# A hybrid decoder block on one core: an own PSUM bank for query, key and mLSTM transposes, another order of the Strassen products in the paired projections, and a pause in the sums of the feed-forward modulation

## The chip, the core and the metric

The kernel runs on one core of a Trainium2 chip. A core has five engines with a queue each: PE (TensorE) multiplies matrices and writes its results to PSUM, DVE (VectorE) and ACT (ScalarE) do elementwise work and move PSUM results to SBUF, POOL (GpSimd) does some elementwise work and SP (SyncE) issues the DMA transfers. Each engine works through its queue in order, and semaphores make one engine wait for another. The metric is the time of one execution on the device, in microseconds (us); lower is better.

## The reference

A decoder block over 2048 tokens of width 1024, all in float32. Cut to what matters:

```python
mod = c @ w_ada + b_ada
shift_m, scale_m, gate_m, shift_f, scale_f, gate_f = split(mod, 6)
h = rms_norm(x, g_pre_mix) * (1 + scale_m) + shift_m
q_a, k_a, v_a, q_m, k_m, v_m, o_m, i_m, f_m, g_a, g_m = split(h @ w_in)
y_a = sliding_window_attention(rope(q_a), rope(k_a), v_a, sinks)      # 8 heads, 2 key heads, window 128
q_m, k_m = split(silu(causal_depthwise_conv([q_m, k_m])))
y_m = sigmoid(o_m) * head_layer_norm(mlstm_chunkwise(q_m, k_m, v_m, i_m + b_i, f_m + b_f))
merged = sigmoid(g_a) * (y_a @ w_branch_attn) + sigmoid(g_m) * (y_m @ w_branch_mlstm)
x = x + gate_m * rms_norm(merged @ w_out, g_post_mix)
h2 = rms_norm(x, g_pre_ffn) * (1 + scale_f) + shift_f
x = x + gate_f * rms_norm((silu(h2 @ w_gate) * (h2 @ w_up)) @ w_down, g_post_ffn)   # width 2816
```

## The kernel before

**Stages.** Phase 1 computes the mixers in two superblocks of two token blocks each (b0 and b1, 512 tokens a block); phase 2 is the feed-forward network over two halves of 1024 tokens. In a superblock the projections of queries, of keys and values (`q_kv`) and of the mLSTM values (`vm`) come first for b0 and then for b1. Then come 14 *pairs*, which are projections of both blocks at once (output gates, mLSTM queries and keys, branch gates), with the mLSTM woven in after the pair ("qk", 3), and then the branch and output projections (`outputs`). Each float32 operand of a large product is split into two parts, hi and lo, and three products of parts make one: `split` makes `whi` on ACT (L256, L259) and `wlo` on DVE (L257, L260) for weights, and the token operands are split by `hprep` (L521 to L537) and `hsums` (L552) for the mixers.

**Pairs.** A pair multiplies a 2 by 2 arrangement of weight quarters with one of token quarters by seven products in place of eight (Strassen, Winograd's form). `PROD` lists the seven in order, each as a weight operand and a token operand (S and T are sums of quarters). `pair_parts` issues them: 12 matmuls of 128x512 a product. Products 0, 2, 4 and 6 accumulate in one PSUM bank X, which is read on the way; products 1, 3 and 5 each take a bank of their own. `combine` evacuates: ACT copies, DVE adds (L1511 and the lines by it). In phase 1 there are 28 pairs, in the feed-forward 44 (22 for each half, gate and up). The `down` projection has its own list, `DOWN`.

**PSUM.** There are eight banks of 128 partitions by 2 KB. Four belong to the tag `acc` (`acc_tile`), four to the tag `mix` (`mix_tile`), from which everything else is served: scores and PV products of attention, all transposes, mLSTM, the second bank of the feed-forward pairs and of `down`. A bank is given again only when what was in it has been read.

**Attention.** `attention(n)` works on one tile of 128 queries. It loads `at`, which holds the queries and keys that `q_stream` and `k_stream` wrote to DRAM (`at_d`). For two halves `jj` it takes two banks, one for each key head `g`; the score matmuls use rows 0 to 63 of the array for one head and 64 to 127 for the other, and are written in alternation. ACT copies (L931) and DVE masks (L933) the scores, DVE and ACT make maxima, exponentials and sums, POOL multiplies by the reciprocal sum (L950), then PE transposes the result and multiplies with the values. `q_stream` and `k_stream` take rotated queries and keys, transpose them into a bank (`pt`), and have ACT and DVE (L772, L798) split them.

**Order.** The program is written with generators: `run2` walks the parts of the main stream, prepares weights ahead of their use, and at each step `tick` moves on the side streams (`spawn`) whose delays have run out on a simulated clock. A framework then schedules the written program onto the engines with a timeline of its own, from tile pools and their free banks, so a changed pool changes the order of instructions on every engine. `ada_stream` (L452) is such a side stream: it computes the modulation vectors, one weight load and one DVE multiply-add (L428) a term, 16 terms a vector. For scale, shift and gate of the feed-forward (48 terms) it starts ahead of the output projection of the first block.

Of the kernel before, what the change touches and what calls it, by code (L numbers as in the profile page):

```python
# [10 lines left out]
F32 = mybir.dt.float32  # L11
# [8 lines left out]
P = 128  # L20
# [30 lines left out]
ADA_AHEAD = (1, 3, 4)  # L51

# [19 lines left out]
def decoder_block(ctx: ExitStack, tc: tile.TileContext, a: dict, out: bass.AP, dbg=None):  # L72
# [26 lines left out]

    def mix_tile():  # L100
        return ps_mix.tile([P, 512], F32, tag="mix", name=nm("mix"))
# [634 lines left out]
    def superblock(sb):  # L736
# [27 lines left out]
        def q_stream(b, t, yz):  # L764
            yield L_ROPE
            y, z = yz
            pt = mix_tile()
# [23 lines left out]
        def k_stream(n, yz):  # L791
            yield L_ROPEK
            y, z = yz
            pt = mix_tile()
# [206 lines left out]
        def chunk_state(c):  # L1001
# [13 lines left out]
            pk = mix_tile()  # L1015
# [26 lines left out]
        def chunk_out(c):  # L1042
# [43 lines left out]
            py = mix_tile()  # L1086
# [124 lines left out]
        def outputs(b):  # L1211
# [41 lines left out]
            def before_out():  # L1253
                if b == 0:
                    finish(R["ada_m"])
                    R_ada.append(spawn(ada_stream([(4, "scale"), (3, "shift"), (5, "gate")], 9000.0)))
# [30 lines left out]
        yield lambda: hps.update(t=spawn(hsums(("T2", "T4"))))  # L1287
# [37 lines left out]
    R_ada = []  # L1325

# [8 lines left out]
    PROD = (("11", "11"), ("12", "21"), ("S2", "T2"), ("22", "T4"), ("S1", "T1"), ("S3", "T3"), ("S4", "22"))  # L1335
# [42 lines left out]
    def h_combine(b2, rows, quarters, sums):  # L1378
# [14 lines left out]
        for k in range(4):  # L1393
            xk = xn
            v = {}
            for j, (half, i) in enumerate(QUADS):
                kk = k + 4 * half
                ps = mix_tile()
# [67 lines left out]
    def pair_parts(w, c0, done, new, spare, bank):  # L1466
# [4 lines left out]
        def make(i, prep):  # L1471
            B = PROD[i][1]

            def mms(wt):
                hi, lo = quad(wt[0]), quad(wt[1])
                if i in IN_X:
                    if i == 0:
                        R["X"] = acc_tile()
                    ps = R["X"]
                else:  # L1480
                    ps = bank()
                for kk in range(4):
                    l, r = (hi[:, kk, :], lo[:, kk, :]), tuple(t[:, kk, :] for t in HC[B])
                    mm(ps, l[0], r[0], kk == 0 and i in (0, 1, 3, 5), False, True)
# [4 lines left out]
            return Part(raw, prep, mms, weave=bank is not mix_tile, ahead=4)  # L1489
# [4 lines left out]
    def combine(i, ps, R, new, done):  # L1494
        if i == 0:
            R["P1"] = new()
            A.copy(R["P1"], ps)
        elif i == 1:
            V.tensor_tensor(R["P1"], ps, R["P1"], op=ALU.add)
            done("11", R["P1"], False)  # L1500
        elif i == 2:
            R["U2"] = new()
            A.copy(R["U2"], ps)
        elif i == 3:
            V.tensor_tensor(R["U2"], ps, R["U2"], op=ALU.add)
        elif i == 4:
            R["U4"] = new()
            A.copy(R["U4"], ps)
        elif i == 5:
            V.tensor_tensor(R["U2"], ps, R["U2"], op=ALU.add)  # L1510
            V.tensor_tensor(R["U4"], ps, R["U4"], op=ALU.add)  # L1511
            done("21", R["U2"], False)
            done("22", R["U4"], False)
# [46 lines left out]
    def gate_up(b2):  # L1560
        late = None
        for p in range(NP):
# [27 lines left out]
            gp, up = (list(pair_parts(w, p * 256, done, unit, unit, mix_tile)) for w, done in ((wg, done_g), (wu, done_u)))  # L1590
# [33 lines left out]
    DOWN = (("11", "11"), ("S3", "T3"), ("S2", "T2"), ("22", "T4"), ("S1", "T1"), ("12", "21"), ("S4", "22"))  # L1624
    HELD = 4

    def down(b2):
# [105 lines left out]
        def make(raw, i, p, j):  # L1733
# [16 lines left out]
            def mms(ab):  # L1750
                if p == 0:
                    for t in range(NT):
                        if i == 0:
                            R[t]["X"] = acc_tile()
                        if i not in IN_X:
                            R[t]["Y"] = mix_tile()
# [113 lines left out]
```

## Time and profile before

| what | value |
|---|---|
| median of 3 runs | 2710.72 us (2709.86 to 2713.3) |
| profiled execution, own time | 2716.59 us |
| its span | 2714.9 us |
| PE busy | 2639.2 us, 97% |
| DVE busy | 1986.2 us, 73% |
| ACT busy | 1299.8 us, 48% |
| DMA | 511.90 MB moved |

The profile is of one execution. It names each instruction by line of the kernel, engine, operation and tiles (out<-in, the numbers of the buffers left out), with partitions and elements and how often it ran. "Idle before" is the time an engine stood before an instruction, and the releaser is what ended that wait. The granted clock is TensorE's, as a share of full speed.

### The profile page before, as it was taken

Reading aid. Unit: us, or ns where it says so; the run is one execution under the profiler, and the core shown is the slowest. Engines: PE = TensorE matmul, PEld = TensorE weight load, DVE = VectorE, ACT = ScalarE, POOL = GpSimd, SP = SyncE. Lnnn points to the kernel's source line nnn. Section 1 sums busy time; section 2 is a strip of 40 time slices with the busy share of each in tenths; the row PEclk is TensorE's granted clock in tenths of the full one; section 3 lists DMA queues with packets and bytes.
Section 4 is the critical chain, followed back from the end, with each engine's and each line's share of the span. In section 5 each row is a group of like instructions: output and inputs, shape, how many; then the busy total and the mean of one; then the engine's idle time right before and its main releaser. Section 6 shows DMA issues by size and latency. Waiting matters only on the chain.

```text
span 2714.9 us, 35793 instructions
## 1 busy us (share of the span) xinstructions
PE 2639.2 (97%) x12310; PEld 2138.9 (79%) x12310; DVE 1986.2 (73%) x3906; ACT 1299.8 (48%) x2558; POOL 148.2 (5%) x189
## 2 busy tenths in 40 slices
PE   6989999999998999999999999999999999999998
PEld 4867788888885678888887888888877888888886
DVE  7968788778695778876687777776677676766456
ACT  5556544444755564444563443335554333333444
POOL 2010001100101000110000000000000000000000
PEclk8999999999998999999999999999999999999999
DMA  7654355897574544678765564436675232324566
GB/s 249 206 184 157 128 172 179 269 340 248 196 235 147 196 138 138 213 231 291 251 224 198 175 201 152 155 113 213 215 271 188 97 117 86 113 97 144 186 210 217
DMA packets 353639, 511.90 MB, mean 189 GB/s; under 512 B 25120, under 2 KB 213660, under 8 KB 348208
## 3 DMA queue, kind: packets, MB, share of 16 engines
q1 hardware_dynamic: 353456, 509.61, 56.9%
q8 instruction: 97, 1.59, 0.2%
q14 instruction: 86, 0.70, 0.1%
HBM read 357.12 MB, written 144.02 MB: 185 GB/s over the span
## 4 chain that ended last, share of the span: by engine, by line
PE 85%; DVE 7%; DMA 4%; ACT 2%; issue 1%; POOL 0%; SPq 0%; DVEq 0%; ACTq 0%; POOLq 0%
PE acc L204 61%; PE mix L204 22%; PE mix L209 2%; DVE hl L1357 1%; DVE tm L428 1%; DMA raw<-as_d 1%; ACT tm L946 1%; ACT hl L1356 1%; DMA raw<-in_w_in_dram 1%; DMA at_d<-tx 0%; DMA big<-in_x_dram 0%; DVE wlo L260 0%; DMA tx<-in_w_ada_dram 0%; DVE w L1667 0%; DMA at<-at_d 0%
## 5 line engine op out<-in xcount | busy, mean ns | idle before, releaser
L204 PE MATMUL acc<-big,hl 128*128 128x512 f32 x3936 | 940.8, 394 | 4.3 <-ACT tx L827 1.8
L204 PEld LDWEIGHTS acc<-big,hl 128*128 128x128 f32 x3936 | 733.3, 188 | 172.5 <-issue 13.8
L1356 ACT CAST hl<-raw 128x512 fp32r<-128x512 f32 x732 | 440.1, 621 | 493.4 <-PE acc L204 222.2
L1357 DVE TENSOR_TENSOR hl<-raw,hl 128x512 fp32r<-128x512 f32 x732 | 496.3, 694 | 194.8 <-ACT hl L1356 194.0
L204 PE MATMUL acc<-whi,big 128*128 128x512 f32 (+1 forms) x1280 | 379.3, 377 | 10.8 <-ACT big L518 8.4
L204 PEld LDWEIGHTS acc<-whi,big 128*128 128x128 f32 x1280 | 236.2, 192 | 52.4 <-ACT big L518 8.5
L204 PE MATMUL mix<-big,hl 128*128 128x512 f32 x1056 | 263.9, 391 | 1.7 <-ACT hl L1356 1.1
L204 PE MATMUL acc<-wlo,big 128*128 128x512 f32 (+1 forms) x640 | 241.2, 379 | 6.4 <-DVE wlo L260 6.4
L204 PE MATMUL acc<-hl,hl 128*128 128x512 f32 x1008 | 237.4, 393 | 5.1 <-DVE hl L1357 3.4
L204 PEld LDWEIGHTS mix<-big,hl 128*128 128x128 f32 x1056 | 197.9, 188 | 45.9 <-ACT hl L1356 1.9
L204 PEld LDWEIGHTS acc<-hl,hl 128*128 128x128 f32 x1008 | 187.0, 188 | 50.9 <-DVE hl L1357 8.8
L204 PE MATMUL mix<-hl,hl 128*128 128x512 f32 x792 | 182.7, 391 | 1.3 <-DVE hl L1357 0.9
L204 PEld LDWEIGHTS mix<-hl,hl 128*128 128x128 f32 x792 | 147.9, 188 | 35.3 <-DVE hl L1357 3.1
L204 PE MATMUL acc<-big,whi 128*128 128x512 f32 x512 | 157.4, 393 | 0.0
L260 DVE TENSOR_TENSOR wlo<-raw,whi 128x1024 fp32r<-128x1024 f32 (+1 forms) x96 | 109.0, 1137 | 65.5 <-ACT whi L259 59.8
L259 ACT CAST whi<-raw 128x1024 fp32r<-128x1024 f32 (+1 forms) x96 | 94.3, 983 | 123.8 <-PE acc L204 110.4
L204 PEld LDWEIGHTS acc<-wlo,big 128*128 128x128 f32 x640 | 123.7, 193 | 28.3 <-DVE wlo L260 8.6
L475 POOL TENSOR_TENSOR rs<-ms,nhalf 128x1 f32<-128x1 f32 (+1 forms) x56 | 42.6, 772 | 1617.5 <-DVE ms L473 1610.5
L204 PE MATMUL mix<-hcT4h,hl 128*128 128x512 f32 x352 | 117.7, 395 | 0.7 <-ACT hl L1356 0.7
L204 PE MATMUL acc<-hcT2h,hl 128*128 128x512 f32 x352 | 117.6, 394 | 0.0
L204 PEld LDWEIGHTS acc<-big,whi 128*128 128x128 f32 x512 | 95.4, 188 | 19.2
L204 PE MATMUL acc<-big,wlo 128*128 128x512 f32 x256 | 97.7, 393 | 0.0
(330 smaller groups left out, 3491.5 us busy)
## 6 DMA issues: line engine op xcount, KB each, us to landing
raw<-in_w_in_dram SPq DMA_DIRECT2D x48, 1024.0 KB
as_d<-w SPq DMA_DIRECT2D x154, 256.0 KB
raw<-as_d SPq DMA_DIRECT2D x70, 512.0 KB
raw<-in_w_ffn_gate_dram SPq DMA_DIRECT2D x22, 1024.0 KB
raw<-in_w_ffn_up_dram SPq DMA_DIRECT2D x22, 1024.0 KB
raw<-ws_d SPq DMA_DIRECT2D x40, 512.0 KB
y_d<-tm SPq DMA_DIRECT2D x64, 256.0 KB
tx<-in_w_ada_dram SPq DMA_DIRECT2D x64, 256.0 KB
```

The source lines that it names most:

```text
L204: T.matmul(o, lhsT=lhsT, rhs=rhs, start=start, stop=stop, skip_group_check=resumed)
L209: T.transpose(o, i, ident[:k, :k])
L259: A.copy(hv, src)
L260: V.tensor_tensor(lv, src, hv.bitcast(F32), op=ALU.subtract)
L428: V.scalar_tensor_tensor(acc, raw[:, k, :], c_, acc, op0=ALU.mult, op1=ALU.add)
L475: G.tensor_tensor(r[:, :n], ms[:, :n], nhalf[:, :n], op=ALU.pow)
L946: A.activation(sc[g][:, j, :], sc[g][:, j, :], AF.Exp, bias=nm_[:, hd:hd + 1], accum_out=sums[:, hd:hd + 1])
L1356: A.copy(v(hi), src)
L1357: V.tensor_tensor(v(lo), src, v(hi).bitcast(F32), op=ALU.subtract)
```

## The change

- `mix_tile` has three banks, and a new `tr_tile` has one (tag `tr`). `q_stream`, `k_stream`, the key transposes of `chunk_state` (`pk`) and the output transposes of `chunk_out` (`py`) use `tr_tile`. The feed-forward uses `any_tile`, which takes the `tr` bank every fourth time and a `mix` bank the other three (token transposes of `h_combine`, the second bank of pairs and of `down`).
- `PROD` gets the order that `DOWN` had. In a pair, product 1 (S3·T3) opens the second bank Y, and product 3 (22·T4) accumulates onto it, so that one evacuation brings the sum of both. Product 5 (12·21) opens Y anew. `combine` has three ACT copies as before and three DVE adds in place of four.
- `hsums` is called for T3 and T2 first, then for T4 and T1 (before: T2 and T4, then T1 and T3).
- The side stream for the feed-forward's scale, shift and gate runs its first 24 terms 6000 ns of simulated clock apart and then waits until the attention of the last block has been started; the other 24 follow 9000 ns apart (before: all 9000 apart, without a pause).

```diff
+ADA_EARLY = 24
...
     def mix_tile():
-        return ps_mix.tile([P, 512], F32, tag="mix", name=nm("mix"))
+        return ps_mix.tile([P, 512], F32, tag="mix", name=nm("mix"), bufs=3)
+
+    def tr_tile():
+        return ps_mix.tile([P, 512], F32, tag="tr", name=nm("tr"), bufs=1)
+
+    def any_tile():
+        turn[0] = (turn[0] + 1) % 4
+        return mix_tile() if turn[0] else tr_tile()
...
-    def ada_stream(parts, gap):
+    def ada_stream(parts, gap, rest=None, go=None):
+        count = 0
         for part, kind in parts:
             for ch in range(2):
                 c0 = part * D + ch * 512
                 acc = tm([P, 512])
                 for k in range(KD):
+                    count += 1
+                    if rest is not None and count > ADA_EARLY:
+                        gap = rest
+                        while not go:
+                            yield rest
...
         def q_stream(b, t, yz):
             yield L_ROPE
             y, z = yz
-            pt = mix_tile()
+            pt = tr_tile()
...
-        yield lambda: hps.update(t=spawn(hsums(("T2", "T4"))))
+        yield lambda: hps.update(t=spawn(hsums(("T3", "T2"))))
...
-            hps["t"] = spawn(hsums(("T1", "T3")))
+            hps["t"] = spawn(hsums(("T4", "T1")))
             attend(b1)
+            if sb:
+                go_on.append(True)
...
-    PROD = (("11", "11"), ("12", "21"), ("S2", "T2"), ("22", "T4"), ("S1", "T1"), ("S3", "T3"), ("S4", "22"))
+    PROD = (("11", "11"), ("S3", "T3"), ("S2", "T2"), ("22", "T4"), ("S1", "T1"), ("12", "21"), ("S4", "22"))
...
-                if i in IN_X:
-                    if i == 0:
-                        R["X"] = acc_tile()
-                    ps = R["X"]
-                else:
-                    ps = bank()
+                if i == 0:
+                    R["X"] = acc_tile()
+                elif i in (1, 5):
+                    R["Y"] = bank()
+                ps = R["X" if i in IN_X else "Y"]
...
-                    mm(ps, l[0], r[0], kk == 0 and i in (0, 1, 3, 5), False, True)
+                    mm(ps, l[0], r[0], kk == 0 and i in (0, 1, 5), False, True)
...
     def combine(i, ps, R, new, done):
-        if i == 0:
-            R["P1"] = new()
-            A.copy(R["P1"], ps)
-        elif i == 1:
-            V.tensor_tensor(R["P1"], ps, R["P1"], op=ALU.add)
-            done("11", R["P1"], False)
...
+        if i in (0, 1, 2):
+            n = ("P1", "Q5", "U2")[i]
+            R[n] = new()
+            A.copy(R[n], ps)
+        elif i in (3, 4, 5):
+            n, qd = {3: ("U2", "21"), 4: ("Q5", "22"), 5: ("P1", "11")}[i]
+            V.tensor_tensor(R[n], ps, R[n], op=ALU.add)
+            done(qd, R[n], False)
```

The order of instructions moves at three places that the prediction speaks of. In the rows, a name and a number stand for one tile; `at` is the loaded attention operand, `tx` holds rotated queries or keys, `tm` softmax results, `ident` is the identity used for transposes, `whi` and `wlo` are split weights and `acc` the bank of a projection, `wlo_1111` one such weight part; "x4" counts equal neighbours. Line numbers are those of each file: L204 and L209 of before are L214 and L219 of after.

**Attention of two tiles in the first superblock, PE.** Before, from the last two score matmuls on (128x256 rows are scores, 64x512 rows are products with the values):

```order
L204 MATMUL mix_1466<-at_1359 128x256
L204 MATMUL mix_1467<-at_1359 128x256
L209 MATMUL mix_1522<-ident,tm_1368 128x128 x4
L209 MATMUL mix_1552<-ident,tm_1369 128x128 x4
L204 MATMUL mix_1567<-tm_1527,at_1328 64x512
L204 MATMUL mix_1567<-tm_1557,at_1328 64x512
L204 MATMUL mix_1567<-tm_1529,at_1328 64x512
L204 MATMUL mix_1567<-tm_1559,at_1328 64x512
L209 MATMUL mix_1578<-ident,tm_1446 128x128 x4
L209 MATMUL mix_1596<-ident,tm_1447 128x128 x4
L204 MATMUL mix_1614<-tm_1583,at_1359 64x512
L209 MATMUL mix_1797<-ident,tx_1704 128x128
```

After, ahead of and between the same softmax transposes (`tm_1368` and `tm_1369`); the last score matmul of these tiles stands 16 rows ahead of the first row shown:

```order
L214 MATMUL acc_1972<-whi_1906,big_666 128x512
L219 MATMUL tr_1985<-ident,tx_1916 128x128 x4
L214 MATMUL acc_1973<-whi_1906,big_665 128x512
L214 MATMUL acc_1973<-wlo_1907,big_665 128x512
L214 MATMUL acc_1973<-whi_1906,big_666 128x512
L214 MATMUL acc_1973<-whi_1906,big_665 128x512
L214 MATMUL acc_1973<-wlo_1907,big_665 128x512
L214 MATMUL acc_1973<-whi_1906,big_666 128x512
L219 MATMUL mix_1522<-ident,tm_1368 128x128 x4
L214 MATMUL acc_1974<-whi_1906,big_665 128x512
L214 MATMUL acc_1974<-wlo_1907,big_665 128x512
L219 MATMUL mix_1552<-ident,tm_1369 128x128 x4
```

In before the transposes of the softmax stand right behind the scores, and the key transposes of b1 (`tx_1704` and on) behind them. After, the key transposes and a query transpose of b1 (`tx_1916`) and projection matmuls stand between scores and softmax transposes.

**Start of the first superblock, PE.** Before, the query transposes of b0 (`tx_654`, `tx_678`, `tx_702`, `tx_720`) together with token transposes (`big`):

```order
L204 MATMUL acc_735<-whi_807,big_421 128x264
L209 MATMUL mix_753<-ident,tx_654 128x128 x4
L209 MATMUL mix_768<-ident,big_534 128x128 x2
L209 MATMUL mix_768<-ident,big_536 128x128 x2
L209 MATMUL mix_776<-ident,tx_678 128x128 x4
L209 MATMUL mix_798<-ident,tx_702 128x128 x4
L209 MATMUL mix_814<-ident,tx_720 128x128 x4
L204 MATMUL acc_732<-wlo_808,big_421 128x264
```

After, around the second of them; the first stands 51 rows ahead of it and the third 25 behind:

```order
L214 MATMUL acc_735<-whi_864,big_422 128x264
L219 MATMUL tr_776<-ident,tx_678 128x128 x4
L214 MATMUL acc_1029<-whi_910,big_335 128x512
L214 MATMUL acc_1030<-whi_910,big_335 128x512
L214 MATMUL acc_1029<-wlo_911,big_335 128x512
```

The four query transposes shared four banks and stood next to each other; now they share one, and some 80 rows, most of them projection matmuls, stand between the first and the last.

**The same place, DVE.** Before, from the third split of the weights that follow the key-value weights (`wlo_1111`) on:

```order
L260 TENSOR_TENSOR wlo_1111<-raw_868,whi_1110 128x1024
L535 TENSOR_TENSOR big_538<-big_539,big_538 128x512
L536 TENSOR_TENSOR big_539<-big_539,big_204 128x512
L759 TENSOR_TENSOR tx_984<-tx_984,cos_479 128x128
L760 TENSOR_TENSOR tx_964<-tx_964,tx_966 128x2x32
L761 TENSOR_TENSOR tx_964<-tx_964,tx_966 128x2x32
L811 COPY v_last<-tx_944 128x128
L835 TENSOR_SCALAR sp_1046<-gt 128x16
```

After, rows that stand ahead of that split:

```order
L788 TENSOR_SCALAR tx_702<-tr_798,tx_704 128x512
L828 TENSOR_TENSOR gt<-tx_964,b_if 128x4
L829 TENSOR_TENSOR gt<-tx_964,b_if 128x4
L826 TENSOR_TENSOR tx_964<-tx_964,v_last 128x128
L827 COPY v_last<-tx_964 128x128
L568 TENSOR_TENSOR big_1548<-big_1548,big_1608 128x512 x4
L788 TENSOR_SCALAR tx_720<-tr_814,tx_722 128x512
L568 TENSOR_TENSOR big_1550<-big_1550,big_1686 128x512
L773 TENSOR_TENSOR tx_966<-tx_964,sin_478 128x2x32
L774 TENSOR_TENSOR tx_966<-tx_964,sin_478 128x2x32
L568 TENSOR_TENSOR big_1550<-big_1550,big_1686 128x512 x2
```

`wlo_1111` stands 16 rows behind the last of these. The sums of `hsums` (L568 after, which is L552 before) all stood behind `wlo_1111` and the three splits after it; now the eight of T3 and T2 stand ahead of it (the last of them two rows further on), between the evacuations of the query transposes (L788 after, L772 before).

More of the change, by code (lines that the diff above doesn't have):

```diff
@@ L1255, in before_out @@
                     finish(R["ada_m"])
-                    R_ada.append(spawn(ada_stream([(4, "scale"), (3, "shift"), (5, "gate")], 9000.0)))
+                    R_ada.append(spawn(ada_stream([(4, "scale"), (3, "shift"), (5, "gate")], 6000.0, 9000.0, go_on)))
                 if b == b1 and b + 1 < NBLK:
@@ L1488, in mms @@
                 combine(i, ps, R, new, done)
-            return Part(raw, prep, mms, weave=bank is not mix_tile, ahead=4)
+            return Part(raw, prep, mms, weave=bank is not any_tile, ahead=4)
         for i, prep in enumerate(a_operands(raw, spare)):
@@ L1494, in combine @@
     def combine(i, ps, R, new, done):
-        if i == 0:
-            R["P1"] = new()
-            A.copy(R["P1"], ps)
-        elif i == 1:
-            V.tensor_tensor(R["P1"], ps, R["P1"], op=ALU.add)
-            done("11", R["P1"], False)
[L1501 to L1513, printed above, removed]
+        if i in (0, 1, 2):
[6 more added lines that the diff above has]
+            done(qd, R[n], False)
         else:
@@ L1588, in a_sums @@
                     nc.sync.dma_start(as_d[b2][:, IDX[n], p, :], t_)
-            gp, up = (list(pair_parts(w, p * 256, done, unit, unit, mix_tile)) for w, done in ((wg, done_g), (wu, done_u)))
+            gp, up = (list(pair_parts(w, p * 256, done, unit, unit, any_tile)) for w, done in ((wg, done_g), (wu, done_u)))
             load, sums = down_weights(p)
```

14 lines of the change are left out of this document (8 added, 6 removed).

## Prediction

> **What bounds the kernel now.** I read the page first (busy time, slices, chain), then the list of PE waits, then tables by stretch, and last the instructions of the stretches that stood out. From the page:
>
> ```profile
> PE 2639.2 (97%) x12310; PEld 2138.9 (79%) x12310; DVE 1986.2 (73%) x3906; ACT 1299.8 (48%) x2558; POOL 148.2 (5%) x189
> ...
> PE 85%; DVE 7%; DMA 4%; ACT 2%; issue 1%; POOL 0%; SPq 0%; DVEq 0%; ACTq 0%; POOLq 0%
> ```
>
> PE, the matmul engine, is busy for 97% of the span of 2714.9 us and carries 85% of the chain that ended last. Work taken off another engine is worth something only where PE waits for it. The stretches that matter, in us (columns: length, then busy time of PE, weight load, DVE, ACT, POOL, then the granted PE clock, DMA share, GB/s):
>
> ```profile
> 75.00:108.00 33.00, 31.45 (x178) 26.88 (x177) 30.98 (x87) 21.00 (x35) 0.00 (x0) 1.00 0.71 217
> 108.00:124.00 16.00, 13.95 (x106) 13.43 (x105) 14.42 (x31) 8.56 (x18) 0.00 (x0) 0.89 0.92 310
> 160.00:185.00 25.00, 18.14 (x92) 9.63 (x92) 13.88 (x40) 15.17 (x54) 4.68 (x5) 0.86 0.39 123
> 400.00:560.00 160.00, 160.00 (x859) 137.11 (x858) 123.03 (x315) 72.94 (x143) 25.16 (x22) 1.00 0.77 244
> 742.00:800.00 58.00, 52.53 (x334) 46.49 (x333) 51.95 (x137) 30.04 (x54) 0.00 (x0) 0.97 0.71 237
> 840.00:867.00 27.00, 18.93 (x86) 10.33 (x87) 13.45 (x40) 14.50 (x53) 4.67 (x5) 0.68 0.32 101
> 867.00:1000.00 133.00, 127.90 (x613) 94.96 (x611) 105.93 (x236) 76.62 (x190) 8.32 (x8) 0.99 0.56 177
> 1445.00:1845.00 400.00, 399.74 (x1756) 327.81 (x1754) 298.45 (x488) 153.67 (x278) 2.16 (x4) 1.00 0.52 167
> 2100.00:2400.00 300.00, 300.00 (x1313) 246.20 (x1313) 205.03 (x329) 104.83 (x185) 0.00 (x0) 1.00 0.32 105
> ```
>
> In the feed-forward rows (1445 on) and in the pair stretch with the mLSTM (400 to 560) PE is busy all the time at full clock: nothing can be won there, only lost. PE's idle time sits in two kinds of place. One is attention on its own, 160 to 185 in the first superblock and 840 to 867 in the second. The other is the start of each superblock, 75 to 124 and 742 to 800, where DVE is the busy engine (30.98 of 33, 51.95 of 58). PE's instructions in the first attention stretch (start, length, operation, tile, shape, count, and in brackets the idle time before):
>
> ```profile
> 163.51 0.97 PE L204 MATMUL mix<-at 64*128 64x256 f32 x6
> 167.22 1.70 PE L204 MATMUL mix<-at 64*128 64x256 f32 x24 [2.75 <-DMA at<-at_d]
> 170.71 1.39 PE L209 MATMUL mix<-ident,tm 128*128 128x128 f32 x8 [1.79 <-DVE tm L933]
> 172.07 4.09 PE L204 MATMUL mix<-tm,at 128*64 128x512 f32 x8
> 177.59 0.65 PE L209 MATMUL mix<-ident,tm 128*128 128x128 f32 x4 [1.42 <-POOL tm L950]
> 179.03 1.04 PE L209 MATMUL mix<-ident,tm 128*128 128x128 f32 x4 [0.79 <-POOL tm L950]
> ```
>
> Scores, transposes of the softmax, PV product, transposes again, and no projection matmul in these rows: PE stands while DVE masks and POOL scales. The projections of the same block follow only behind them.
>
> **The change part by part.**
>
> *The own bank, at the attention of b1.* In before, query and key transposes of b1 take mix banks behind the attention that holds them, and the value projection waits behind those. In the changed order, projection matmuls and query and key transposes stand between the scores and the softmax transposes of these tiles, in both superblocks. What that fills: in 160 to 185 the idle time is 25 − 18.14 = 6.9 us, and the slow clock costs 18.14 × (1 − 0.86) = 2.5, together 9.4. In 840 to 867 it is 27 − 18.93 = 8.1 and 18.93 × 0.32 = 6.1, together 14.2. I take all of it, −23.6. Least gain: half of it, −11.8, if the load of `at` (2.75 above) still ends last; most: another 5.1, the idle time of 867 to 1000.
>
> The Trainium skill, "TensorE: Matmul & The Clock Gate", section "HAM oscillation — how this bites in real kernels", says that only PE pauses beyond about 3.4 us drop the clock. In 160 to 185 the longest quoted pause is 2.75 and the clock is 0.86, so the trace doesn't bear the limit out; by the rule those 2.5 us would come from something else and stay, and the sum below would be 2.5 higher.
>
> *Fewer mix banks, at the scores.* Two score groups run side by side on the two halves of the array when they alternate: 24 of them took 1.70 us, and six of one group 0.97. One's own length is about 0.28 (the second of the three times, least, median and most in ns, in the last row below; the first row is the feed-forward's and starts at 1413.2), so alternating ones come every (1.70 − 0.28)/23 = 0.062 us, others every (0.97 − 0.28)/5 = 0.138.
>
> ```profile
> L204 PE MATMUL mix<-big,hl x1056: 387/390/500, 1413.2 to 2485.6; 128*128 128x512 f32 x176
> ...
> L204 PE MATMUL mix<-at x384: 268/279/580, 122.6 to 967.3; 64*128 64x256 f32 x180, 64*128 64x128 f32 x12
> ```
>
> With three banks the scheduler writes 154 neighbouring pairs of different groups where it wrote 239. 85 × 0.076 = **+6.5 us**. Ends: 0, if PE waits there for the masks anyway, and the 6.5.
>
> The skill's same page, Part 3 "Packing small matmuls — row/col tiling", has matmuls on different rows of the array start some 4 ns apart, which speaks against the change; by the widths here its model would give an estimate of +4.6.
>
> *One bank, at the start of a superblock.* Four query streams of b0 now share the one bank, each waiting for the evacuation of the one before, so they spread out, and in their place the scheduler pulls DVE work of the next block's sums ahead. Counted in DVE's order up to the third weight split (L260) after the key-value weights, the first superblock has eight more L552, two more L536, two L537 and one L535. These stood behind that split:
>
> ```profile
> L552 DVE TENSOR_TENSOR big<-big,big 128x512 fp32r<-128x512 f32 x8 | 5.1, 668 | 0.0
> L537 DVE TENSOR_TENSOR big<-big,big 128x512 f32<-128x512 f32 x2 | 1.4, 687 | 0.0
> L536 DVE TENSOR_TENSOR big<-big,big 128x512 f32<-128x512 f32 x2 | 1.4, 682 | 0.0
> ...
> L535 DVE TENSOR_TENSOR big<-big,big 128x512 f32<-128x512 f32 x1 | 0.7, 683 | 0.0
> ```
>
> That is 5.1 + 1.4 + 1.4 + 0.7 = 8.6 us ahead of weights that PE waits for, on an engine busy 94% of that stretch, so all of it goes on the path. Given back is the wait that this work caused later:
>
> ```profile
> 117.70 0.59 PE L204 MATMUL acc<-wlo,big 128*128 128x264 f32 x1 [2.05 <-DVE wlo L260]
> ```
>
> That one goes, and with it 2.05: 8.6 − 2.1 = **+6.5**. The second superblock moves the same eight and five. There the pause of the shift and scale sums takes four terms (L428) out of the stretch, and PE's waits for the splits at its end shrink (their total, count and longest in the second view):
>
> ```profile
> L428 DVE SCALAR_TENSOR_TENSOR tm<-tx,c_sb,tm 128x512 f32<-128x512 f32 x4 | 3.0, 742 | 0.0
> ...
> L772 DVE SCALAR_TENSOR_TENSOR tx<-mix,tx 128x512 fp32r<-128x512 f32 x4 | 2.8, 689 | 0.0
> ```
>
> ```profile
> PE acc L204 <- DVE wlo L260: 3.2, 5, 1.3
> ```
>
> 8.6 − 3.0 − about two thirds of 3.2 = **+3.5**. Ends for both starts together: 0 (DVE had room after all, by its idle 2.0 and 6.0 us there) and 8.6 + 5.6 = 14.2.
>
> *The query and key bank elsewhere.* `pk` and `py` of the mLSTM use it too, one after the other. They lie in a stretch with PE at 160.00 of 160 us, covered by pair matmuls in the order: 0. If that cover failed, each would cost an evacuation like L772's 0.69.
>
> *The pairs.* The new order has one DVE add in place of two for 22·T4, 72 fewer in all:
>
> ```profile
> L1511 DVE TENSOR_TENSOR w<-mix,w x44: 684/692/693, 1440.4 to 2489.4; 128x512 f32<-128x512 f32 x44
> L1511 DVE TENSOR_TENSOR tx<-acc,tx x28: 676/682/692, 227.2 to 1226.3; 128x512 f32<-128x512 f32 x28
> ```
>
> 44 × 0.692 + 28 × 0.682 = 49.5 us of DVE, off the path: PE is busy 399.74 of 400 with DVE at 75%. Worth 0; at most the 0.3 us idle per 400 us, say 1, and at worst +3 if held tiles (the first copy now lives five products, not one) stop a product. T4 is needed a product sooner; three products of 12 matmuls at 300/1313 = 0.228 us, 8.2 us, cover its four adds of 0.67. PE's matmul count doesn't change.
>
> *The pause.* 48 weight loads of the shift, scale and gate vectors move; the first half comes closer together, the rest waits for the attention of the last block. The last term of before is 1129.8 us into the span; by the order it goes some 50 us of PE work later, and the feed-forward starts at 1413.2 (row above). SP issues the loads with nothing that waits behind them at the new place. 0 beyond the 3.0 already counted.
>
> ```profile
> L428 DVE SCALAR_TENSOR_TENSOR tm<-tx,c_sb,tm x56: 653/746/1542, 319.7 to 1129.8; 128x512 f32<-128x512 f32 x56
> ```
>
> **Sum.** −23.6 + 6.5 + 6.5 + 3.5 + 0 = −7.1 us. The profiled execution took 2716.59, so 2709.5; its own time is 5.9 above the median 2710.72 of the runs, and against that the forecast is **2703.6 us**.
>
> **Rivals.** What a measurement here tells from no change is about 0.2%, 5.4 us.
>
> *The starts cost little.* For it: DVE's order is packed by the scheduler, and the pulled work must be done some time; PE is behind DVE by little at 75 (31.45 of 33 busy). Then only −23.6 + 6.5 = −17.1, 2693.6.
>
> *About no change.* The starts cost in full, 14.2, and nothing comes back: −23.6 + 6.5 + 14.2 = −2.9, 2707.8. For it: in both starts DVE is over 89% busy. Against: PE does show waits there that this work caused.
>
> *Slower: the single bank holds PE up.* Query and key transposes of b1 now stand in PE's queue ahead of the softmax transposes, 32 streams in all with the starts, and each needs the one before evacuated by ACT and DVE and its own rotary sums done on DVE. PE is in order, so each such wait stops the scores, the projection and all else behind it. With one L772 (0.69) of wait each it is 32 × 0.69 = +22, 2725.6. It decides for slower from (7.1 + 5.4)/32 = 0.39 us each. Against: between two of them now lie several matmuls of projection in the order.
>
> **Chances.** Forecast 0.42, starts cheap 0.22, no change 0.16, slower 0.20. Faster by over 0.2% is below 2705.3, where some 0.33 of the forecast's 0.42 lie (its own range is 2697 to 2709): 0.33 + 0.22 = 0.55; same 0.09 + 0.16 = 0.25; slower 0.20. The range takes in the first three cases, a little below the second for the 5.1 us that might come on top, and half of the slower one: 2690 to 2720.
>
> **What would show it.** Right: no PE wait above 1 us for the masks (L933) or the scaling (L950) in the attention of b1, clock 1.0 there; PE ending the products of the third split weight some 6 to 9 us later than before in the first superblock; feed-forward length unchanged; 72 fewer DVE adds. Wrong: PE waits for ACT or DVE on the new transposes, more than 0.39 us each; a feed-forward phase that differs from before by over 3 us; the start of a superblock not longer at all.

## The result, and the profile after

The changed kernel is slower: 2745.91 us (median of 4 runs, 2744.58 to 2747.18) against 2711.38 of before on the same chip, a ratio of 1.0126 (95% interval 1.0111 to 1.0141), some 34 us. The forecast was 2703.6, with a range of 2690 to 2720. Its profiled execution took 2744.84 us, 28.3 more than the one of before that the prediction counted from (that one was itself 5.9 us above its median).

The page of the changed kernel, its summary and its chain, and PE's longest waits (engine, tile, line, what it waited for: us in total, times, longest):

```profile
PE 2661.4 (97%) x12310; PEld 2150.6 (78%) x12310; DVE 1960.7 (71%) x3834; ACT 1305.0 (48%) x2558; POOL 154.7 (6%) x189
...
PE 85%; DVE 7%; DMA 3%; ACT 2%; issue 1%; SPq 0%; POOL 0%; DVEq 0%; POOLq 0%; ACTq 0%
```

```profile
PE acc L214 <- ACT tx L822: 10.8, 5, 3.1
PE acc L214 <- ACT big L534: 8.0, 3, 4.0
...
PE acc L214 <- DVE wlo L270: 4.9, 3, 3.4
...
PE mix L214 <- DVE cl L899: 3.3, 1, 3.3
...
PE mix L219 <- POOL tm L966: 1.3, 2, 0.9
```

The list of before has these two for attention:

```profile
PE mix L209 <- DVE tm L933: 5.9, 2, 4.1
PE mix L209 <- POOL tm L950: 5.4, 6, 1.4
```

DVE has the 72 operations fewer that were foreseen. The waits for POOL in attention have gone from 5.4 to 1.3 us, and those for the masks (L933 of before) aren't among the longest any more. At the top of the list stands a wait that isn't on the list of before: PE for `ACT tx L822`, the copy that evacuates a key-value tile (L806 in before).

Windows of the changed kernel, with the columns of the table of before:

```profile
75.00:132.00 57.00, 43.30 (x218) 34.95 (x216) 43.70 (x115) 27.99 (x49) 0.00 (x0) 0.88 0.61 198
132.00:150.00 18.00, 18.00 (x78) 16.04 (x79) 8.48 (x26) 7.25 (x26) 2.08 (x2) 0.53 0.20 56
150.00:185.00 35.00, 35.00 (x187) 25.36 (x187) 22.22 (x82) 19.54 (x53) 2.25 (x2) 1.00 0.71 217
770.00:835.00 65.00, 52.97 (x300) 45.46 (x299) 53.36 (x142) 31.47 (x54) 0.00 (x0) 0.90 0.56 176
835.00:900.00 65.00, 65.00 (x346) 48.55 (x345) 43.28 (x134) 34.86 (x105) 6.70 (x6) 1.00 0.54 171
2100.00:2400.00 300.00, 300.00 (x1312) 245.79 (x1312) 203.71 (x316) 105.80 (x187) 0.83 (x2) 1.00 0.33 113
```

Attention is full now (35.00 of 35 us, 65.00 of 65, clock 1.00). The starts of both superblocks are what got long: PE idle 13.7 us of 57 from 75 to 132, then at half clock for 18 us, and idle 12.0 of 65 from 770 to 835. From 75 to 132 DVE too is busy for only 43.70 of the 57 us, so it doesn't set the pace throughout. The feed-forward runs as before.

To compare kernels whose order differs I counted PE's *loss*: from each matmul's start to the start of the next, less the usual distance for its shape (227 ns for 128x512 in two-part products, 121 for 128x264, and so on), added up along PE's order. Side-by-side scores give a small negative loss. The usual work is 2602 us in every kernel here, so stretches set by work done are the same in all. Loss by stretch of PE work, in us:

| kernel | 0–50 | 50–120, first start | 120–300, attention | 300–640 | 640–660 | 660–780, second start | 780–950, attention | 950–1300 | 1300–1400 | 1400–2600, feed-forward | sum |
|---|---|---|---|---|---|---|---|---|---|---|---|
| before | 27.2 | 3.4 | 7.2 | 0.8 | 0.2 | 8.9 | 18.3 | 1.1 | 5.3 | 21.9 | 103.3 |
| after | 31.1 | 23.5 | 3.0 | 1.5 | 7.6 | 22.7 | 1.4 | 1.8 | 6.4 | 23.7 | 131.5 |
| difference | +3.9 | +20.1 | −4.2 | +0.7 | +7.4 | +13.8 | −16.9 | +0.7 | +1.1 | +1.8 | +28.2 |

(Sums are of unrounded numbers.) So the two starts took 34 us, attention gave back 21, and 7.4 us were lost at a place that the prediction doesn't name. The 3.9 us of the first column belong to the first start too: 50 us of work are done some 80 us into the run. Which usual distance the small shapes are given shifts the edge between the first two columns. With the median distance of each shape in before, up to 6 us more of the loss falls into the second column where the query transposes of b0 share the single bank, while the two columns together change by under 1 us (+23.4 where the table has +24.0). So read these two together.

What the first start loses is of two kinds. The same stretch of work, some 50 to 120 us of it by those medians, in before and in the changed kernel (columns as above):

```profile
78.00:153.00 75.00, 72.38 (x420) 61.58 (x421) 63.86 (x193) 46.01 (x107) 4.70 (x4) 0.98 0.67 211
77.00:176.00 99.00, 86.14 (x417) 68.51 (x418) 67.10 (x202) 48.27 (x115) 4.33 (x4) 0.84 0.56 175
```

PE's idle time grew from 2.6 to 12.9 us, and the slow clock costs 86.14 × 0.16 = 13.8 us where it cost 72.38 × 0.02 = 1.4. So waiting is less than half of the price; the slow clock that comes with it is the rest.

The chain of the changed kernel in the first start (start, length, what):

```profile
90.47 1.13 DVE wlo L270
91.60 0.60 DVE tx L788
92.21 0.60 DVE big L551
92.99 6.61 DMA at_d<-tx
99.68 0.39 ACT tx L822
100.11 4.26 PE acc L214 x12
104.37 0.82 PE tr L219 x4
105.22 0.61 ACT tx L787
```

Up to 92.9 it goes through DVE: weight splits and token sums (L551, L553), some of them pulled ahead. The eight L568 that were pulled ahead with them (102.75 to 109.42) aren't on it. From 93.0 it goes through a store of a query stream (`at_d<-tx`), the evacuation of a key-value tile, and PE. The store matters since it frees a tile. A query stream holds two tiles of the `tx` pool, from its evacuation until its store has ended; four streams hold eight of nine. The evacuation of a key-value tile takes two. ACT's rows show it:

```profile
85.65 0.59 ACT L787 ACTIVATE tx<-tr 128x512 fp32r<-128x512 f32 x1
87.38 0.38 ACT L822 COPY tx<-acc 128x264 f32<-128x264 f32 x1 [1.13 <-DMA at_d<-tx]
97.61 0.60 ACT L787 ACTIVATE tx<-tr 128x512 fp32r<-128x512 f32 x1 [9.85 <-PE tr L219]
99.68 0.38 ACT L822 COPY tx<-acc 128x264 f32<-128x264 f32 x1 [1.48 <-DMA at_d<-tx]
105.22 0.60 ACT L787 ACTIVATE tx<-tr 128x512 fp32r<-128x512 f32 x1 [0.94 <-PE tr L219]
107.78 0.38 ACT L822 COPY tx<-acc 128x264 f32<-128x264 f32 x1
```

One query transpose (L787 is its copy) and one key-value evacuation (L822) alternate, each 8 to 12 us behind the last of its kind. With one bank the streams can only end one after the other; each that ends frees tiles for one evacuation, which frees one accumulation bank, which lets PE go on to the next transpose. That was the theory to test.

### The profile page after: what moved, and what is told of

Read it like the earlier page. It is cut to its first block, busy times and chain, and to the rows that moved or that the text cites. A ratio compares the mean times of both kernels' runs of the same rounds, so it can differ in the third digit from the quotient of the medians.

```text
span 2743.1 us, 35705 instructions
## 1 busy us (share of the span) xinstructions
PE 2661.4 (97%) x12310; PEld 2150.6 (78%) x12310; DVE 1960.7 (71%) x3834; ACT 1305.0 (48%) x2558; POOL 154.7 (6%) x189
## 4 chain that ended last, share of the span: by engine, by line
PE 85%; DVE 7%; DMA 3%; ACT 2%; issue 1%; SPq 0%; POOL 0%; DVEq 0%; POOLq 0%; ACTq 0%
PE acc L214 61%; PE mix L214 20%; PE tr L214 3%; DVE hl L1376 1%; PE mix L219 1%; DVE tm L438 1%; PE tr L219 1%; ACT hl L1375 1%; DMA at_d<-tx 1%; DMA raw<-as_d 1%; DVE wlo L270 0%; DMA raw<-ws_d 0%; DMA x<-tx 0%; DVE big L1376 0%; DVE w L1674 0%
## 5 line engine op out<-in xcount | busy, mean ns | idle before, releaser
L214 PE MATMUL acc<-big,hl 128*128 128x512 f32 x3936 | 944.9, 392 | 4.2 <-ACT tx L1516 2.1
L214 PEld LDWEIGHTS acc<-big,hl 128*128 128x128 f32 x3936 | 731.3, 188 | 171.8 <-issue 9.9
L214 PE MATMUL acc<-whi,big 128*128 128x512 f32 (+1 forms) x1280 | 395.2, 387 | 21.0 <-ACT tx L822 10.8
L214 PEld LDWEIGHTS acc<-whi,big 128*128 128x128 f32 x1280 | 243.2, 198 | 72.5 <-ACT tx L822 11.9
L214 PE MATMUL acc<-wlo,big 128*128 128x512 f32 (+1 forms) x640 | 247.2, 388 | 4.9 <-DVE wlo L270 4.9
L214 PE MATMUL acc<-hl,hl 128*128 128x512 f32 x1008 | 237.4, 393 | 4.7 <-DVE hl L1376 3.8
L214 PEld LDWEIGHTS acc<-hl,hl 128*128 128x128 f32 x1008 | 187.0, 188 | 50.2 <-DVE hl L1376 9.2
L214 PE MATMUL mix<-big,hl 128*128 128x512 f32 x792 | 201.4, 390 | 1.7 <-DVE hl L1376 1.0
L214 PEld LDWEIGHTS mix<-big,hl 128*128 128x128 f32 x792 | 148.4, 188 | 34.3 <-DVE hl L1376 1.4
L214 PE MATMUL mix<-hl,hl 128*128 128x512 f32 x594 | 157.4, 391 | 3.0 <-ACT hl L1375 1.9
L214 PE MATMUL acc<-big,whi 128*128 128x512 f32 x512 | 158.0, 394 | 0.0
L214 PEld LDWEIGHTS acc<-wlo,big 128*128 128x128 f32 x640 | 127.0, 198 | 31.7 <-DVE wlo L270 6.3
L214 PEld LDWEIGHTS mix<-hl,hl 128*128 128x128 f32 x594 | 110.7, 188 | 29.4 <-ACT hl L1375 4.0
L214 PE MATMUL mix<-hcT4h,hl 128*128 128x512 f32 x352 | 117.6, 394 | 1.7 <-ACT w L1516 1.7
L214 PE MATMUL acc<-hcT2h,hl 128*128 128x512 f32 x352 | 117.7, 395 | 1.2 <-ACT w L1516 1.2
L214 PEld LDWEIGHTS acc<-big,whi 128*128 128x128 f32 x512 | 95.0, 188 | 19.5 <-issue 0.5
L214 PE MATMUL acc<-big,wlo 128*128 128x512 f32 x256 | 97.8, 392 | 0.0
```

What stands on the lines that cost most here:

```text
L214: T.matmul(o, lhsT=lhsT, rhs=rhs, start=start, stop=stop, skip_group_check=resumed)
```

## Experiments

Each kernel was timed over three rounds beside the kernel before. Ratios carry a 95% interval.

**The own bank alone, and the rest alone.** `tr_only` is the kernel before with the bank; `no_tr` is the changed kernel without it.

```diff
 # tr_only, against before
-        return ps_mix.tile([P, 512], F32, tag="mix", name=nm("mix"))
+        return ps_mix.tile([P, 512], F32, tag="mix", name=nm("mix"), bufs=3)
+    def tr_tile():
+        return ps_mix.tile([P, 512], F32, tag="tr", name=nm("tr"), bufs=1)
...
 # no_tr, against the changed kernel
-        return ps_mix.tile([P, 512], F32, tag="tr", name=nm("tr"), bufs=1)
+        return mix_tile()
```

> The own bank alone: the kernel before, with three mix banks, the one-bank tag for query, key and mLSTM transposes, and the feed-forward taking the four banks in turn; old order of products, old order of the sums, no pause. Theory 1 (the single bank holds the query streams of b0, and with them two tx tiles each of nine, so that the key-value evacuations and through them PE stand): the start of both superblocks is 30 to 40 us longer as in the changed kernel, attention 15 us shorter, in all 2735 to 2752 us. Theory 2 (the other parts of the change cost most of it): within 8 us of before, 2705 to 2720.

> The changed kernel with the own bank taken back (all on four mix banks): the new order of products, the new order of the sums and the pause stay. Theory 1: no long start, no gain in attention, 2703 to 2718 us, and what it differs from before is the price of those three parts. Theory 2: 2735 or more.

`tr_only` took 2722.51 us, 1.0042 (1.0028 to 1.0057); `no_tr` 2718.47, 1.0029 (1.0017 to 1.0041). Neither theory had the size of `tr_only`, and `no_tr` ends 0.5 us above the range of its theory 1: the bank alone costs a third of the change. By stretch its starts lose 14.7 and 20.9 us (3.4 and 8.9 before) and attention 0.7 and 1.0 (7.2 and 18.3), and the first column has 5.0 more. The other parts cost 8 us by themselves, and together the two cost more than their sum: 34 against 12 + 8.

The traces say where the surplus at the first start comes from. The same stretch in `tr_only`, with its longest wait there, and then the two longest of the changed kernel (77 to 176):

```profile
79.00:169.00 90.00, 79.70 (x425) 61.65 (x426) 66.35 (x202) 48.53 (x117) 4.17 (x4) 0.94 0.63 200
```

```profile
PE acc L213 <- ACT tx L815: 6.2, 3, 2.5
```

```profile
PE acc L214 <- ACT tx L822: 6.2, 3, 2.5
PE mix L214 <- DVE cl L899: 3.3, 1, 3.3
```

The bank alone already makes the wait for the key-value evacuation (L815 there), to the tenth. `tr_only` is idle for 10.3 us and loses 79.70 × 0.06 = 4.8 to the slow clock. What the changed kernel has on top is one wait of 3.3 us for a mix bank that DVE empties of gate transposes (L899), and behind it the 18 us at half clock, 8.5 us: together 11.8, which covers the 9 us between the two windows (99 and 90 us). In the changed kernel the terms of the pause start at 340.0 us and the first pair is copied at 224.1, so of the other parts the order of the sums is the likeliest behind that wait; no run here takes it alone.

**Query transposes back on the mix banks.**

```diff
         def q_stream(b, t, yz):
...
-            pt = tr_tile()
+            pt = mix_tile()
```

> The changed kernel, but query transposes go back to the mix banks (three now); key and mLSTM transposes keep the own bank. Theory 1: query streams of b0 run three wide, the waits of PE for the key-value evacuation go from 10.8 us to under 4, the start is 20 us or more shorter, 2705 to 2726 us. If the chain were that of the key and mLSTM transposes in one bank: no more than 5 us better, 2740 to 2747.

2708.04 us, 0.999 (0.998 to 0.9999): 38 us better by one line, as theory 1 expected. The starts lose 3.4 and 5.0 us, and the wait for L822 isn't on PE's list any more.

**The tiles.** In `kv_tm` both tiles of a key-value evacuation come from the `tm` pool, in `q_z_tm` each query stream of b0 takes one of its two tiles from it. The single bank stays in both.

```diff
 # kv_tm
-                raw = tx([P, 392])
+                raw = tm([P, 512])[:, :392]
...
-            z = tx([P, 512])
+            z = (tm if heads == HKV else tx)([P, 512])
 # q_z_tm
-            z = tx([P, 512])
+            z = (tm if heads == HQ and b % 2 == 0 else tx)([P, 512])
```

> The changed kernel with one difference: keys and values of a tile are evacuated into the tm pool and not the tx pool, so that the eight tx tiles that four query streams hold can't stop them. The single bank stays. Theory 1, if the tiles are the link: PE no longer waits for the key-value evacuation, 15 us or more shorter, 2715 to 2732 us. If the single bank itself holds PE up (PE in order behind each transpose): at most 5 us better, 2740 to 2750.

> The changed kernel, with one of the two tiles of each query stream of b0 (the rotation's second) taken from the tm pool, so that the streams hold four tx tiles in place of eight; the single bank stays. Theory 1a (the waiting streams stop the key-value evacuation by their tiles): PE's wait for that evacuation (10.8 us in five) goes under 4, the loss of the first start (23 us in the changed kernel) falls to 12 or less and stays away in attention, in all 2715 to 2732 us. Theory 1b (the bank holds PE up whatever the tiles): the first start loses 20 us or more, 2740 to 2750. If the tiles' shortage only moves into the tm pool, as with keys and values in it: start short, attention of the first superblock 10 us or more longer, 2735 to 2750.

`kv_tm` took 2748.74 us, 1.0141 (1.0126 to 1.0156), so by its time the tiles would be acquitted. Its waits say otherwise (PE's list):

```profile
PE mix L219 <- POOL tm L966: 15.0, 10, 6.3
...
PE mix L214 <- DMA at<-at_d: 4.4, 3, 1.9
...
PE acc L214 <- ACT tm L822: 2.8, 4, 1.0
```

The wait for the evacuation fell from 10.8 to 2.8 us, and by the median distances 90 us of PE work are begun at 127.1 us, where the changed kernel needs 143.2 and before 122.8. But then attention, which lives on the same `tm` pool, stands for its own softmax (15.0 us in both superblocks together), and 120 us of work are done at 179.9, against 176.3 and 153.0. So the time was lost again in the next stretch. That the `tm` pool is what attention lacks there fits the waits, but it isn't shown. `q_z_tm` splits the tiles between the pools: 2726.99 us, 1.0051 (1.0032 to 1.007), in the range of theory 1a and 19 us better than the changed kernel. It loses 9.9 and 15.0 us at the starts (23.5 and 22.7) and keeps attention at 4.8 and 2.8. Its first start in the windows of above, and its wait there for the evacuation:

```profile
78.00:163.00 85.00, 77.60 (x414) 62.87 (x412) 63.45 (x197) 47.00 (x111) 4.17 (x4) 0.92 0.65 211
```

```profile
PE acc L214 <- ACT tx L822: 0.9, 2, 0.6
```

The wait falls from 6.2 to 0.9 us, PE's idle time from 12.9 to 7.4 and the cost of the slow clock from 13.8 to 77.60 × 0.08 = 6.2. So the tiles are the link for that wait, and without their shortage somewhat more than half of the added time goes: 14 of 24 us at the first start by these windows (99, 85 and 75 us long), 7.7 of 13.8 at the second by the table. More than half of the gain at the first start is slow clock that went with the waits. What stays, the tiles don't explain.

**The pause and the order of products.** `ada_old` is the changed kernel without the pause; `pairs_only` is the kernel before with the new order of products and sums alone.

```diff
 # ada_old
-... ada_stream([(4, "scale"), (3, "shift"), (5, "gate")], 6000.0, 9000.0, go_on)))
+... ada_stream([(4, "scale"), (3, "shift"), (5, "gate")], 9000.0)))
```

> The changed kernel with the shift and scale sums as before (all 48 terms 9000 apart, no pause). Theory 1 (the first 24 terms, closer together, put DVE behind their weight loads just where the first sums of the second superblock need it): the 7.3 us that the changed kernel loses there (PE work 640 to 660 us) go, some 3 us of relief later go too, 2737 to 2742 us. Theory 2 (that loss is from the new order of products): 2744 to 2748.

> The kernel before with the new order of products and of the sums alone: no own bank, no pause; 72 DVE adds fewer. Theory 1 (those adds were hidden, the order costs nothing): 2708 to 2713 us, and the 8 us that the changed kernel without its bank lost come from the pause. Theory 2 (the new order costs): 2715 to 2720. A gain from the adds would be 2700 or less.

`ada_old` took 2755.42 us, 1.016 (1.0145 to 1.0175): without the pause it is 9.5 us slower still, and both theories fell. The place was right: the loss from 640 to 660 is 7.6 us with the pause and its earlier first terms, and 0.4 without. DVE's rows of the changed kernel there:

```profile
712.32 0.75 DVE L438 SCALAR_TENSOR_TENSOR tm<-tx,c_sb,tm 128x512 f32<-128x512 f32 x1 [1.85 <-DMA tx<-in_w_ada_dram]
714.52 0.69 DVE L537 TENSOR_TENSOR big<-big,big 128x512 fp32r<-128x512 f32 x1 [1.46 <-ACT big L536]
715.96 0.75 DVE L438 SCALAR_TENSOR_TENSOR tm<-tx,c_sb,tm 128x512 f32<-128x512 f32 x1 [0.75 <-DMA tx<-in_w_ada_dram]
```

DVE does stand for terms whose weights haven't landed (1.85 and 0.75 us), as theory 1 said. But the token operand's split between them (L537) waits for ACT, and the chain of the changed kernel goes through ACT, which evacuates token transposes from 713.04 to 717.17 (L534 and L536), and from there:

```profile
717.17 0.93 ACT whi L269
718.10 1.18 ACT big L612 x4
719.28 0.69 DVE big L613
720.02 8.17 PE acc L214 x22
```

So the loss comes and goes with the earlier terms, but by what way isn't shown. What the terms cost here they pay back: without the pause the second start, the second attention and the stretch ahead of the feed-forward lose 3.0, 3.7 and 6.1 us more.

`pairs_only` took 2723.08 us, 1.0044 (1.0029 to 1.0059): the order that I had costed at nothing costs 12 us. It loses 11.3 at the first start (3.4), 15.3 from 1300 to 1400 (5.3), 23.4 in the feed-forward (21.9), and gains 11.8 in the second start and attention. The large item is one wait, at the first feed-forward pair. PE's wait there, and ACT's row:

```profile
PE acc L214 <- ACT w L1516: 8.2, 1, 8.2
```

```profile
1430.99 0.59 ACT L1516 COPY w<-acc 128x512 f32<-128x512 f32 x1 [6.90 <-DMA x<-tm]
```

The first copy out of bank X of phase 2 waits 6.90 us for a store of phase 1 (`x<-tm`), so its target `w` seems to lie in memory that phase 1 still holds. Product 2 goes into bank X again, so PE needs that copy. In before products of another pair stand between on PE, and it waits for such a copy (L1503) 0.7 us at most. With the pause (`no_tr`) this stretch loses 4.8. Nor is it the order alone: `q_b1_po` (below) has the old order, and there the same first copy waits for the same store:

```profile
1412.30 0.59 ACT L1516 COPY w<-acc 128x512 f32<-128x512 f32 x1 [5.67 <-DMA x<-tm]
```

PE stands 3.0 us for it there, and 1.2 us in `q_mix_ada` (below), which has the new order and no pause. So how late that store ends seems to decide; on what it depends, these runs don't show.

**Query streams of b0 alone out of the bank.**

```diff
-            pt = tr_tile()
+            pt = tr_tile() if b % 2 else mix_tile()
```

> The changed kernel with the query transposes of b0 alone on the mix banks; those of b1 stay in the own bank. Theory 1 (the price lies at the start of the superblocks, where four query streams of b0 come at once): as without any query stream in the bank, 2703 to 2714 us. If the query streams of b1 ahead of attention cost as well: 2715 to 2735.

> The changed kernel with all query transposes on the mix banks and without the pause. If the two costs add: 2708 less 4 to 7, 2700 to 2704 us, faster than before. If the pause only shows where the bank delays things: 2706 to 2710.

`q_b1` took 2697.56 us, 0.9949 (0.9934 to 0.9964), 13.5 us faster than before and below the range that theory 1 gave. The query streams of b1 cost nothing in the bank; by standing there they fill attention, whose windows of before now read:

```profile
160.00:185.00 25.00, 25.00 (x141) 18.67 (x138) 18.10 (x42) 13.24 (x37) 2.09 (x2) 1.00 0.66 226
840.00:867.00 27.00, 27.00 (x156) 21.67 (x156) 19.65 (x42) 17.68 (x47) 2.08 (x2) 1.00 0.78 260
```

`q_mix_ada`, all query transposes on the mix banks and no pause, took 2711.24 us, 0.9999 (0.9989 to 1.0009): some 3 us more than with the pause, though the two intervals overlap; the two costs don't add.

**The bank without the other parts, and the parts one by one beside it.** `bank_b1` is the kernel before with the bank as in `q_b1`, and nothing else; `q_b1_e9` is `q_b1` with the first 24 terms 9000 apart; `q_b1_po` is `q_b1` with the old order of products and sums.

> The kernel before with the own bank alone, used by the query streams of b1, the key streams and the mLSTM, with the query streams of b0 on the mix banks; old order of products and sums, no pause. Theory 1 (the bank wins in attention and loses only by the query streams of b0): the own bank for all took 2722.5; the two starts give back 11 and 15 us, 2692 to 2702 us. If the bank's loss is spread over all its users: 2710 to 2720.

> The changed kernel with the query transposes of b0 on the mix banks (2697.6) and with the first 24 shift and scale terms 9000 apart as before, then the pause. Theory 1 (the closer spacing puts DVE behind weight loads at the first sums of the second superblock, 6 us): 2689 to 2695 us. If the gain of the pause hangs on the terms being early: 2698 to 2706.

> The changed kernel with the query transposes of b0 on the mix banks and with the old order of products and sums (so 72 DVE adds more); the pause stays. Theory 1 (the new order alone cost 12 us: at the second block's products, at the start of the feed-forward and 1 to 2 us along it): 2684 to 2693 us. If the new order costs nothing beside the bank: 2695 to 2702. If its fewer adds gain there: 2703 or more.

They took 2695.07 us, 0.9931 (0.9915 to 0.9948), 2700.35, 0.9952 (0.9937 to 0.9967), and 2699.53, 0.9953 (0.9939 to 0.9968). `bank_b1` is in the range of theory 1, though the starts give back 8 and 9 us and attention gains the rest. It has the lowest time here, 17 us under before and 51 under the changed kernel; from `q_b1` its interval doesn't part it. Beside a bank that doesn't stall, the pause, the closer terms and the order of products make no difference that these intervals can tell, and theory 1 of both `q_b1_e9` and `q_b1_po` (6 us and more from undoing them) fell. In `q_b1_e9` the 6.3 us from 640 to 660 do go (0.4), but the second start takes them back (14.4 against 5.8).

| kernel | median us | first start | attention | 640–660 | second start | attention | 1300–1400 |
|---|---|---|---|---|---|---|---|
| before | 2711 | 3.4 | 7.2 | 0.2 | 8.9 | 18.3 | 5.3 |
| after | 2746 | 23.5 | 3.0 | 7.6 | 22.7 | 1.4 | 6.4 |
| `tr_only` | 2723 | 14.7 | 0.7 | 0.2 | 20.9 | 1.0 | 5.3 |
| `no_tr` | 2718 | 6.8 | 7.8 | 6.3 | 3.2 | 11.9 | 4.8 |
| `pairs_only` | 2723 | 11.3 | 8.0 | 0.2 | 4.1 | 11.3 | 15.3 |
| `ada_old` | 2755 | 25.4 | 4.6 | 0.4 | 25.7 | 5.1 | 12.5 |
| `q_mix` | 2708 | 3.4 | 1.5 | 6.3 | 5.0 | 5.3 | 4.5 |
| `q_z_tm` | 2727 | 9.9 | 4.8 | 7.1 | 15.0 | 2.8 | 8.1 |
| `kv_tm` | 2749 | 27.8 | 0.3 | 6.2 | 27.9 | 0.4 | 5.8 |
| `q_b1` | 2698 | 6.3 | −0.8 | 6.3 | 5.8 | −3.8 | 6.1 |
| `bank_b1` | 2695 | 6.8 | −4.4 | 0.2 | 11.5 | −0.1 | 5.2 |

At the first start `tr_only` loses 8.8 us less than the changed kernel, and `pairs_only`, which has the new order of the sums, 7.9 more than before. The two fit each other, and in `pairs_only` too it is slow clock in the main (from 78 to 161 us PE is idle for 5.1 and loses 77.93 × 0.08 = 6.2 to the clock). No run here takes the order of the sums alone.

## Why the prediction was wrong

*What bounds the kernel, and attention.* Right. The own bank filled both attention stretches; the terms −23.6 and +6.5, together −17.1, measured −4.2 − 16.9 = −21.1. The split over the two was off: the first attention gave half of its 9.4. The lost alternation of scores can't be read apart from it.

*One bank, at the start of a superblock.* This is the step that failed. The prediction took +6.5 and +3.5, with 14.2 for both as the upper end; they measured +20.1 and +13.8. Sums that were pulled ahead are on the chain there, up to 92.9 us, so part of that exists. But the eight L568, 5.1 of the 8.6 us, aren't on it, DVE stood idle for 13.3 of 57 us, and the third weight split itself began 14.9 us later (at 111.67, before at 96.76), where 6 to 9 were foreseen for the end of its products. I charged the streams' waiting in line only by the DVE work that took its place, and never asked what a stream holds while it waits. It holds two of nine `tx` tiles, the key-value evacuations need the same pool, PE needs their banks, and the next transpose stands behind PE: 6.2 us of waits at the first start, 0.9 with the tiles split (`q_z_tm`). More than half of the price came as slow clock (below). The pulled work goes with the tiles held: in `q_mix` and `kv_tm` the order has the sums behind the third weight split again.

*The bound from both sides* was therefore no bound: both ends came from rows of DVE, and the cost came by way of ACT and a pool.

*The clock.* I counted the slow clock where it was to vanish and not where new waits would bring it. At the first start it costs 13.8 us (1.4 before), a term that the prediction doesn't have. From 132 to 150 PE is busy all the time at 0.53, 18.00 × 0.47 = 8.5 us, behind a single wait:

```profile
131.99 1.22 PE L214 MATMUL mix<-at 64*128 64x128 f32 x6 [3.26 <-DVE cl L899]
```

The prediction weighed the Trainium skill, "TensorE: Matmul & The Clock Gate", section "HAM oscillation — how this bites in real kernels", and found its limit of about 3.4 us not borne out. That holds: a wait of 2.05 us in before is followed by a slow clock (below). The prediction didn't use the warning in it: a gap of about that size, 3.26 us, stands right ahead of the longest slow stretch.

*The pairs, at nothing.* Wrong by the runs: 12 us alone, though no difference that the intervals tell beside the bank without the queries of b0. The 72 adds show no gain, as said. The largest part of the cost, 10.0 us, lies where one pair's first copy meets the end of phase 1, in a stretch that the prediction left out, taking two windows of the steady feed-forward (from 1445 on) for all of it. In the feed-forward itself the change measured +1.8, inside the +3 given.

*The pause, −3.0.* Its sign was right: 9.5 us in the changed kernel, and 4.6 and 3 in two more pairs of kernels whose intervals overlap. In the changed kernel the second start loses 3.0 us less with it, as costed. What the prediction left out are the earlier terms, which cost 7.4 us from 640 to 660.

*The rivals.* The third, that the single bank holds PE up, has the right bank and the right sign; its 2725.6 us and 0.2 were too little. It named the streams of b1 ahead of attention first, and `q_b1` shows that these cost nothing. "The starts cost little", at 0.22, was refuted by the same runs.

## What to carry to other kernels

When a change gives fewer banks to a group of streams, write down what each stream holds while it waits for its turn (tiles, banks, places in a queue), and who else draws on that pool; here the price was paid there, and in the slow clock behind the waits, not on the engine that does the streams' work. A shared resource can win in one stretch and lose in another by the same edit: price each group of users by itself, and try the edit for one group at a time, as `bank_b1` does. An experiment that moves a shortage to another pool can leave the time as it was and still show that link, if the waits are read by stretch.

## What the hardware showed that I had not expected

The clock falls after shorter waits than I had thought to matter, and stays down for unequal times. In before, a wait of 2.05 us at 117.7 is followed by three microseconds at half clock:

```profile
113.00:118.00 5.00, 2.95 (x23) 0.97 0.97 266
118.00:121.00 3.00, 3.00 (x15) 0.50 1.01 365
```

(Columns: length, PE busy, clock, DMA share, GB/s.) In the changed kernel the wait of 3.26 us at 132 is followed by 18 us at 0.53, with PE busy throughout. Why the second lasted six times as long, these runs don't show.
